# Cached keys of an attention step turned by VectorE in square blocks instead of by TensorE

## The chip, the cores and the metric

The kernel runs on one core of a Trainium2 chip. The metric is the device time of one execution in microseconds (us). The time before is the median of three runs. A profile was recorded by the hardware profiler on one more execution, whose own time is given beside its span. The engines are called PE (TensorE, the matmuls), PEld (its weight loads), DVE (VectorE), ACT (ScalarE), POOL (GpSimd) and SP (the engine that issues most transfers).

## The reference, cut to what matters

One inference step of a hybrid layer: one input projection, whose columns go to eight heads of attention and to a gated short convolution, then an output projection with a residual, then a gated feed-forward part with a residual. 512 new prompt frames and 64 frames of a running stream pass through it. The 64 sample frames also see 512 cached keys and values per head, and only this part of the attention is touched:

```python
# q: (B,Tq,H,Dh), k and v: (B,Tk,H,Dh); 8 heads of 128; 512 cached keys ahead of the 64 new ones
def stick_breaking(q, k, v, q_pos, k_pos):
    z = jnp.einsum('bqhd,bkhd->bhqk', q, k) / math.sqrt(HEAD_DIM)
    mask = (k_pos[None, :] < q_pos[:, None])[None, None]
    log_1mb = jnp.where(mask, jax.nn.log_sigmoid(-z), 0.0)
    after = lax.cumsum(log_1mb, axis=3, reverse=True) - log_1mb
    w = jnp.where(mask, jnp.exp(jax.nn.log_sigmoid(z) + after), 0.0)
    return jnp.einsum('bhqk,bkhd->bqhd', w.astype(v.dtype), v)

k_all = jnp.concatenate([k_past, k], axis=1)     # cache_k: (1, 1, 512 frames, 8 heads, 128)
```

The cached keys lie in memory with the frame as the row. To be multiplied with the queries on TensorE, which contracts over partitions, they must stand with the head's 128 dimensions on the partitions: they have to be turned.

## The kernel before

All matrices are split into a high and a low part (`split`, L228 the cast on ScalarE, L229 the rest on VectorE), and a projection matmul group is three matmuls (`whi` times high, `wlo` times high, `whi` times low).

Attention runs beside the output projection of the convolution's half (`out_proj(mixed_conv, ...)`). Two loops are interleaved. The outer one (`product`, L220) walks over the projection matmuls and calls `pipe.tick()` after every three. The inner one is a Python generator, `attend(h)`, that emits a piece of head h and then yields a number of ticks until its next piece is to be emitted. `heads()` starts a new head every 29 ticks (`PERIOD`), so the end of head h overlaps the start of head h+1.

The order on TensorE is just this order of emission (`manual_schedule` for PE). The order on VectorE, ScalarE, GpSimd and SP is made by the scheduler from dependences and its own cost model, unless `tc.issue_after(x)` holds an instruction behind x.

The pieces of one head, by ticks from its start:

- 0 to 6: the scores `z2`, `z1`, `z0` of the prompt frames against the prompt keys in blocks; on each `softplus` (three ScalarE passes L1131 to L1133 and one VectorE pass L1134 into `pr` or `hbl`), the mask and a running sum on GpSimd (L1189, L1195), and splits into `ph`/`pl`, `s1h`/`s1l`, `s0h`/`s0l`.
- 7: `zs`, the scores of the 64 sample frames (L1204): first one block of new keys from `kf`, then four blocks of cached keys from `kcT`. Behind it `softplus`, and on GpSimd a mask, a copy and three running sums (L1208 to L1212).
- 16: `keys_cached(h + 1)`: TensorE turns the next head's cached keys `cK`, in four 128x128 transposes (matmuls with the identity, L1157) into a PSUM bank `kc`; ScalarE copies the bank to `kcT` (L1158); then the load of the keys after those is issued on SP (`load_cached_keys`, L1042). For head 0 `keys_cached(0)` stands between the scores `z1` and `z0`.
- 18 to 31: the sums over later keys and the weights (`weights`), the split of `sp` into `sph` and `spl` (read by `sample_weights`, L1219, L1220), and the mixed output `po` in PSUM.
- 34, which is tick 5 of the next head: `mixed(po, 0, TP)`. ScalarE makes the high part `hi` of the mixed output and VectorE the low part `lo` (L1274), both parts of the tile `mixa`. ScalarE then squares `po` for the norm.

So TensorE reads `kcT` of head h+1 two ticks behind the last matmul into `po` of head h, and there is one buffer each of `cK` and `kcT`.

## Time and profile before

| | before |
|---|---|
| time, median of 3 runs | 2329.69 us (2328.64 to 2332.22) |
| the profiled execution's own time | 2329.59 us |
| its span in the profile | 2327.9 us |
| PE busy | 2315.9 us (99%) |
| DVE busy | 1956.4 us (84%) |
| ACT busy | 1221.5 us (52%) |
| POOL busy | 298.1 us (13%) |
| granted TensorE clock | 1.00 |
| transfers | 368.57 MB, 158 GB/s in the mean |
| transposes into `kc` on PE | 32, from 584.0 to 716.5 us, 272 ns median |
| copies `kcT` from `kc` on ACT | 8, from 585.6 to 718.1 us, 578 ns median |

The span is the time from the first to the last instruction; the profiled execution's own time has 1.7 us around it. Busy time is the sum over an engine's instructions. Durations of matmuls are modelled and overlap, so what a matmul costs TensorE is read from the distance of the starts. "A <- B" in a row of waits means that A waited for B; "out<-in" in other rows is the tile that an instruction writes and those that it reads.

### The profile page before, as it was taken

Reading aid. Unit: us, or ns where it says so; the run is one execution under the profiler, and the core shown is the slowest. Engines: PE = TensorE matmul, PEld = TensorE weight load, DVE = VectorE, ACT = ScalarE, POOL = GpSimd, SP = SyncE. Lnnn points to the kernel's source line nnn. Section 1 sums busy time; section 2 is a strip of 40 time slices with the busy share of each in tenths; the row PEclk is TensorE's granted clock in tenths of the full one; section 3 lists DMA queues with packets and bytes.
Section 4 is the critical chain, followed back from the end, with each engine's and each line's share of the span. In section 5 each row is a group of like instructions: output and inputs, shape, how many; then the busy total and the mean of one; then the engine's idle time right before and its main releaser. Section 6 shows DMA issues by size and latency. Waiting matters only on the chain.

```text
span 2327.9 us, 43552 instructions
## 1 busy us (share of the span) xinstructions
PE 2315.9 (99%) x17432; PEld 2306.7 (99%) x17432; DVE 1956.4 (84%) x2871; ACT 1221.5 (52%) x2170; POOL 298.1 (13%) x374
## 2 busy tenths in 40 slices
PE   9999999999999999999999999999999999999999
PEld 8999999999999999999999999999999999999999
DVE  8889989897777898888888888888888777887897
ACT  8556656456887564444444444444444444444443
POOL 0211121110332320000000000000000002431222
PEclk9999999999999999999999999999999999999999
DMA  8444343546643454444444444345344936885654
GB/s 272 136 118 130 91 142 109 145 131 209 192 144 108 162 204 127 155 139 140 150 134 150 133 146 155 116 152 158 116 155 136 349 129 211 222 242 186 205 137 100
DMA packets 533770, 368.57 MB, mean 158 GB/s; under 512 B 70278, under 2 KB 518016, under 8 KB 533568
## 3 DMA queue, kind: packets, MB, share of 16 engines
q1 hardware_dynamic: 527072, 356.45, 48.9%
q0 software_dynamic: 6384, 9.21, 2.2%
q8 instruction: 136, 2.23, 0.4%
q14 instruction: 66, 0.54, 0.1%
q10 hardware_dynamic: 112, 0.14, 0.0%
HBM read 285.52 MB, written 80.23 MB: 157 GB/s over the span
## 4 chain that ended last, share of the span: by engine, by line
PE 93%; ACT 3%; DVE 2%; DMA 1%; issue 0%; POOL 0%; SPq 0%; POOLq 0%; ACTq 0%; DVEq 0%
PE psy L405 47%; PE psw L405 23%; PE psx L405 12%; PE pjo L224 6%; PE pj L691 1%; PE pjz L691 1%; PE psv L405 1%; PE pjm L691 1%; DMA raw_a<-in_w_down_dram 0%; ACT ph L228 0%; PE psx L556 0%; ACT whi L176 0%; DVE whl L229 0%; DMA raw_b<-in_w_down_dram 0%; DMA vtok<-v_dram 0%
## 5 line engine op out<-in xcount | busy, mean ns | idle before, releaser
L229 DVE TENSOR_TENSOR whl<-raw_a,whl 128x1024 fp32r<-128x1024 f32 (+4 forms) x384 | 432.8, 1128 | 55.0 <-ACT whl L228 53.4
L405 PE MATMUL psy<-t,whl 128*128 128x288 f32 x3000 | 447.2, 294 | 0.0
L228 ACT CAST whl<-raw_a 128x1024 fp32r<-128x1024 f32 (+4 forms) x384 | 360.0, 939 | 139.9 <-PE psx L405 45.3
L405 PE MATMUL psy<-h_s,whl 128*128 128x288 f32 x2766 | 416.4, 294 | 0.6 <-ACT part L428 0.6
L405 PEld LDWEIGHTS psy<-t,whl 128*128 128x128 f32 x3000 | 414.3, 188 | 0.0
L405 PE MATMUL psw<-t,whl 128*128 128x288 f32 x2688 | 388.9, 294 | 0.0
L405 PEld LDWEIGHTS psy<-h_s,whl 128*128 128x128 f32 x2766 | 383.1, 188 | 0.9 <-ACT part L428 0.8
L405 PEld LDWEIGHTS psw<-t,whl 128*128 128x128 f32 x2688 | 366.7, 188 | 0.0
L228 ACT CAST whl<-raw_b 128x1024 fp32r<-128x1024 f32 (+5 forms) x234 | 211.4, 905 | 209.9 <-issue 71.4
L229 DVE TENSOR_TENSOR whl<-raw_b,whl 128x1024 fp32r<-128x1024 f32 (+5 forms) x234 | 253.2, 1082 | 72.7 <-ACT whl L228 71.6
L428 ACT COPY part<-psy 128x288 f32<-128x288 f32 x309 | 123.2, 399 | 346.6 <-PE psy L405 343.2
L405 PE MATMUL psx<-h_s,whl 128*128 128x288 f32 x1164 | 170.2, 294 | 0.0
L228 ACT CAST whl<-s 128x1024 fp32r<-128x1024 f32 (+5 forms) x103 | 95.3, 925 | 123.5 <-PE psw L405 116.0
L405 PEld LDWEIGHTS psx<-h_s,whl 128*128 128x128 f32 x1164 | 159.6, 188 | 0.0
L405 PE MATMUL psy<-t12a,whl 128*128 128x288 f32 x1056 | 150.5, 295 | 0.0
L405 PE MATMUL psw<-t34a,whl 128*128 128x288 f32 x1056 | 150.4, 295 | 0.0
L405 PEld LDWEIGHTS psy<-t12a,whl 128*128 128x128 f32 x1056 | 143.3, 188 | 0.4 <-ACT part L428 0.2
L405 PEld LDWEIGHTS psw<-t34a,whl 128*128 128x128 f32 x1056 | 143.5, 188 | 0.0
L1454 POOL DMA_DIRECT2D hid_dram<-form x7 | 5.2, 738 | 951.7 <-DVE form L229 944.5
L229 DVE TENSOR_TENSOR whl<-s,whl 128x1024 fp32r<-128x1024 f32 (+5 forms) x103 | 110.4, 1071 | 19.2 <-ACT whl L228 18.2
L224 PE MATMUL pjo<-mixc,whi 128*128 128x288 f32 x512 | 119.0, 300 | 0.0
L224 PE MATMUL pjo<-mixa,whi 128*128 128x288 f32 x512 | 102.8, 296 | 0.0
(565 smaller groups left out, 3920.8 us busy)
## 6 DMA issues: line engine op xcount, KB each, us to landing
hid_dram<-form SPq DMA_DIRECT2D x147, 288.0 KB
raw_a<-in_w_in_dram SPq DMA_DIRECT2D x22, 1024.0 KB
raw_b<-in_w_in_dram SPq DMA_DIRECT2D x22, 1024.0 KB
raw_b<-in_w_gate_dram SPq DMA_DIRECT2D x22, 1024.0 KB
raw_b<-in_w_up_dram SPq DMA_DIRECT2D x22, 1024.0 KB
raw_a<-in_w_gate_dram SPq DMA_DIRECT2D x22, 1024.0 KB
raw_a<-in_w_up_dram SPq DMA_DIRECT2D x22, 1024.0 KB
h_s<-hid_dram SPq DMA_DIRECT2D x10, 2016.0 KB
```

Source lines behind the costliest of these rows:

```text
L224: mm(ps, w_[:, k, csl], x_[:, a:b], start=(k == 0 and n == 0), stop=(k == nk - 1 and n == 2))
L228: cast = nc.scalar.copy(out=hi, in_=src)
L229: (lo_eng or nc.vector).tensor_tensor(out=lo, in0=src, in1=hi.bitcast(F32), op=ALU.subtract)
L405: mm(ps, whl[:, w_, j, :], x_, start=(start and j == 0 and q == 0), stop=(j == len(xs_) - 1 and q == 2), skip_group_check=True)
L428: nc.scalar.copy(out=t, in_=st["y"])
L691: mm(banks_[c][i], w3[:, kt % 8, c * P : (c + 1) * P], t[:, x_, :], start=(kt == 0 and n == 0), stop=(kt == KD - 1 and n == 2))
L1454: q.dma_start(out=hid_dram[fp][2 * n - 2 : 2 * n].rearrange("f p t -> p f t"), in_=t.bitcast(F32))
```

## The change

The keys are loaded in another arrangement. The 512 cached keys of a head are cut into 16 groups of 32 frames and the 128 dimensions into four groups of 32. Row g+j of `cK` holds, for frame j of each of the 16 groups, the 32 dimensions from g on. That takes four transfers per head, each of pieces of 32 numbers (128 bytes), in place of one with pieces of 128 numbers (512 bytes). One VectorE instruction then turns each 32x32 block in itself (`nc.vector.transpose`, a STREAM_TRANSPOSE of 128x512), and what comes out is `kcT` as before. The transposes on TensorE, the bank `kc` and the copy on ScalarE are gone.

The place changes too. For head 0 the keys are turned ahead of the loop over heads. For head h+1 they are turned directly behind VectorE's low part of the mixed output of head h (tick 34 of head h, tick 5 of head h+1), held there by `issue_after`. The load of the next keys stands where `keys_cached` stood.

```diff
-    cK = bpool.tile([P, 4, P], F32, name="cK")
+    cK = bpool.tile([P, TP], F32, name="cK")
...
     def load_cached_keys(h):
-        nc.sync.dma_start(out=cK, in_=ck[:, h, :].rearrange("(i p) d -> p i d", p=P))
+        for g in range(0, P, BK):
+            nc.sync.dma_start(out=cK[g : g + BK].rearrange("j (t d) -> j t d", d=BK),
+                              in_=ck[:, h, g : g + BK].rearrange("(t j) d -> j t d", j=BK))
...
+    nc.vector.transpose(out=kcT, in_=cK)
+
...
-    def keys_cached(h):
-        kc = ps_pj.tile([P, 512], F32, tag="pj", name="kc")
-        for i in range(4):
-            nc.tensor.transpose(kc[:, i * P : (i + 1) * P], cK[:, i, :], ident)
-        nc.scalar.copy(out=kcT, in_=kc)
-        if h + 1 < NH:
-            load_cached_keys(h + 1)
...
             yield 3 if b else 1
-            if h == 0 and b == 1:
-                keys_cached(0)
...
         yield 1
         if h + 1 < NH:
-            keys_cached(h + 1)
+            load_cached_keys(h + 1)
         yield 2
...
         def mixed(ps, a, b):
             nc.scalar.activation(out=hi[:, a:b], in_=ps, func=AF.Copy, scale=ga)
-            nc.vector.scalar_tensor_tensor(out=lo[:, a:b], in0=ps, scalar=ga, in1=hi[:, a:b].bitcast(F32),
-                                           op0=ALU.mult, op1=ALU.subtract)
+            return nc.vector.scalar_tensor_tensor(out=lo[:, a:b], in0=ps, scalar=ga, in1=hi[:, a:b].bitcast(F32),
+                                                  op0=ALU.mult, op1=ALU.subtract).ins
...
-        mixed(po, 0, TP)
+        behind = mixed(po, 0, TP)
+        if h + 1 < NH:
+            with tc.issue_after(behind):
+                nc.vector.transpose(out=kcT, in_=cK)
```

What the change moves on the engines that the scheduler orders is shown at two places. The first is VectorE at the passage from head 1 to head 2. `hbl<-z` is the last pass of a softplus of head 2, `mixa` the low part of head 1's mixed output, `pl` and `s0l` low parts of splits for head 2, `x_2` an output of the projection. Before:

```order
L1134 TENSOR_SCALAR hbl<-z_7309,hbl 128x384
L1274 TENSOR_SCALAR mixa_6730<-po,vec,mixa_6730 128x512
L229 TENSOR_TENSOR pl_6705<-hbl,ph_6704 128x384
L229 TENSOR_TENSOR s0l<-hbl,s0h 128x384
L1104 TENSOR_TENSOR x_2_6737<-pjo,accc 128x288
```

After, at the same place:

```order
L1136 TENSOR_SCALAR hbl<-z_7301,hbl 128x384
L1268 TENSOR_SCALAR mixa_6733<-po,vec,mixa_6733 128x512
L1286 STREAM_TRANSPOSE kcT<-cK 128x512
L229 TENSOR_TENSOR pl_6705<-hbl,ph_6704 128x384
L229 TENSOR_TENSOR s0l<-hbl,s0h 128x384
```

The block transpose has come in between the mixed output and the two splits.

The second place is head 0. On ScalarE, `hbl<-z` and `hbl<-hbl` 128x384 are the softplus passes of key block 1, those on `pr_6700` of key block 0, `hbl<-zs` and `hbl<-hbl` 128x320 those of the sample frames, `whi` weight casts, and `ph_6704`, `ph_6702` and `s0h` the high parts for key block 1, key block 0 and the running sum. Before:

```order
L1131 ACTIVATE hbl<-z_6835 128x384
L1131 ACTIVATE pr_6700<-z_6867 128x512
L1132 ACTIVATE hbl<-hbl 128x384
L1132 ACTIVATE pr_6700<-pr_6700 128x512
L1133 ACTIVATE hbl<-hbl 128x384
L1133 ACTIVATE pr_6700<-pr_6700 128x512
L1131 ACTIVATE hbl<-zs 128x320
L176 COPY whi_6913<-raw_a 128x512
L228 COPY ph_6704<-hbl 128x384
```

After:

```order
L176 COPY whi_6910<-raw_a 128x512 x2
L1133 ACTIVATE hbl<-z_6839 128x384
L228 COPY ph_6702<-pr_6700 128x512
L1134 ACTIVATE hbl<-hbl 128x384
L1133 ACTIVATE hbl<-zs 128x320
L1135 ACTIVATE hbl<-hbl 128x384
L1134 ACTIVATE hbl<-hbl 128x320
L176 COPY whi_6910<-raw_a 128x512
L1135 ACTIVATE hbl<-hbl 128x320
L228 COPY ph_6704<-hbl 128x384
L176 COPY whi_6910<-raw_a 128x512
L228 COPY s0h<-hbl 128x384
```

The softplus of block 1 has moved behind that of block 0 and is interleaved with the sample's, and `ph_6704` and `s0h` stand behind both.

On GpSimd in head 0, L1189 (after: L1185) is the mask, L1195 (L1191) the running sum that `s0h` is cut from, and L1208, L1210 and L1212 (L1202, L1204 and L1206) are the sample's mask, copy and three running sums. Before:

```order
L1189 TENSOR_TENSOR hbl<-hbl,m_6692 128x128
L1189 TENSOR_TENSOR pr_6700<-pr_6700,m_6692 128x128
L1116 DMA x_0_6727<-xt_dram 128x2x576
L1195 TENSOR_TENSOR hbl<-hbl,pr_6701 128x256
L1208 TENSOR_TENSOR hbl<-hbl,s_6694 128x64
L1210 COPY hbl<-hbl 128x64
L1212 TENSOR_TENSOR hbl<-hbl 128x64 x3
```

After:

```order
L1185 TENSOR_TENSOR pr_6700<-pr_6700,m_6692 128x128
L1118 DMA x_0_6730<-xt_dram 128x2x576
L1185 TENSOR_TENSOR hbl<-hbl,m_6692 128x128
L1202 TENSOR_TENSOR hbl<-hbl,s_6694 128x64
L1204 COPY hbl<-hbl 128x64
L1206 TENSOR_TENSOR hbl<-hbl 128x64 x2
L1191 TENSOR_TENSOR hbl<-hbl,pr_6701 128x256
L1206 TENSOR_TENSOR hbl<-hbl 128x64
```

The running sum for `s0h` has moved behind the sample's mask, copy and two of its three sums.

## The prediction

> **What bounds the kernel now.** I read the page first, then the busy time by stage, then TensorE's waits inside the stage that the change touches, then the time line at the places that it moves. The page's head and its chain of waits:

> ```profile
> span 2327.9 us, 43552 instructions
> ...
> PE 2315.9 (99%) x17432; PEld 2306.7 (99%) x17432; DVE 1956.4 (84%) x2871; ACT 1221.5 (52%) x2170; POOL 298.1 (13%) x374
> ...
> PE 93%; ACT 3%; DVE 2%; DMA 1%; issue 0%; POOL 0%; SPq 0%; POOLq 0%; ACTq 0%; DVEq 0%
> ```

> TensorE (PE) is busy for 99% of the span and carries 93% of the chain that ends last. So two things count: matmul time that goes away, and moments in which TensorE has to stand still. Attention runs from about 575 to 750 us. Busy time by stretch (PE, PEld, DVE, ACT, POOL, then clock, DMA share and GB/s); the third row lies in the final stores and is used further down:

> ```profile
> 575.00:605.00 30.00, 29.65 (x219) 29.02 (x218) 20.42 (x41) 22.77 (x50) 7.72 (x14) 1.00 0.95 289
> 605.00:750.00 145.00, 143.22 (x1045) 138.54 (x1044) 109.58 (x232) 116.36 (x264) 50.04 (x92) 1.00 0.42 122
> 2305.00:2310.00 5.00, 5.00 (x40) 5.00 (x39) 5.00 (x8) 2.56 (x5) 1.61 (x2) 1.00 0.20 33
> ```

> Here too TensorE stands still for only 2.1 us of 175, at a granted clock of 1.00, while VectorE (DVE) and ScalarE (ACT) have a quarter of their time free. The waits of TensorE over 575 to 755 us are three rows (total us, times, longest):

> ```profile
> PE zs L1220 <- DVE spl L229: 1.3, 4, 0.4
> PE zs L1204 <- ACT kcT L1158: 0.3, 1, 0.3
> PE zs L1219 <- ACT sph L228: 0.3, 1, 0.3
> ```

> So the cached keys are late once, by 0.3 us, in the first head. In the seven others `kcT` was ready well before its use: no wait for it stands in the view.

> **What it removes.** Eight times four transposes on TensorE and the copy out of PSUM on ScalarE. TensorE's time line around one of the eight (start, duration, operation):

> ```profile
> 590.64 0.30 PE L224 MATMUL pjo<-mixc,whi 128*128 128x288 f32 x1
> 590.78 0.60 PE L1157 MATMUL kc<-ident,cK 128*128 128x128 f32 x4
> 591.13 0.38 PE L224 MATMUL pjo<-mixc,whi 128*128 128x288 f32 x1
> 591.34 0.30 PE L224 MATMUL pjo<-mixc,wlo 128*128 128x288 f32 x1
> ...
> L1158 ACT COPY kcT<-kc x8: 564/578/587, 585.6 to 718.1; 128x512 f32<-128x512 f32 x8
> ```

> A projection matmul takes a slot of 0.14 us (590.64 to 590.78). Without the four transposes the `whi` row would start at 590.78 and the `wlo` row at 590.92; it starts at 591.34. One group costs 0.42 us, eight cost 3.4 us, all on the path: **-3.4 us**. The 0.58 us ScalarE copies (the last row, eight times) are no direct gain, since ScalarE is not what ends last; they loosen the 1.6 us of waits for `sph` and `spl` in the rows above. I take half of that, **-0.8** (bounds 0 and -1.6). In head 0 VectorE turns the keys with no PSUM trip, so the 0.3 us wait goes: **-0.3**.

> **What it adds on VectorE.** Eight block transposes of 128x512. None of that size stands in the trace; the nearest rows are one size below and one above:

> ```profile
> L1607 DVE STREAM_TRANSPOSE acc<-acc x14: 464/469/475, 2272.1 to 2316.8; 128x288 f32<-128x288 f32 x14
> ...
> L807 DVE STREAM_TRANSPOSE tok<-E-18_2212 x1: 769/769/769, 202.6 to 202.6; 128x576 f32<-128x576 f32 x1
> ```

> On the line between 0.469 us at 288 and 0.769 us at 576 columns, 512 columns take 0.70 us (bounds 0.47 and 0.77). Eight are 5.6 us on an engine with room. As busy time they cost nothing. [...]

> **Where the turning now stands.** This is the main term. Before, the keys of head h+1 were turned in the middle of head h. Now VectorE turns them directly behind the mixed output of head h (L1274 in the rows), and TensorE reads `kcT` (L1204) a few slots after the last matmul of that output. Both rows at each of the seven passages from a head to the next:

> ```profile
> 606.63 1.06 PE L1204 MATMUL zs<-qf,kcT 128*128 128x64 f32 x8
> 607.23 0.74 DVE L1274 SCALAR_TENSOR_TENSOR mixa<-po,vec,mixa 128x512 fp32r<-128x512 f32 x1
> 627.00 0.75 DVE L1274 SCALAR_TENSOR_TENSOR mixa<-po,vec,mixa 128x512 fp32r<-128x512 f32 x1
> 627.25 1.06 PE L1204 MATMUL zs<-qf,kcT 128*128 128x64 f32 x8
> 648.66 0.75 DVE L1274 SCALAR_TENSOR_TENSOR mixa<-po,vec,mixa 128x512 fp32r<-128x512 f32 x1
> 648.98 1.06 PE L1204 MATMUL zs<-qf,kcT 128*128 128x64 f32 x8
> 669.38 0.75 DVE L1274 SCALAR_TENSOR_TENSOR mixa<-po,vec,mixa 128x512 fp32r<-128x512 f32 x1
> 669.94 1.06 PE L1204 MATMUL zs<-qf,kcT 128*128 128x64 f32 x8
> 690.79 0.75 DVE L1274 SCALAR_TENSOR_TENSOR mixa<-po,vec,mixa 128x512 fp32r<-128x512 f32 x1
> 691.27 1.06 PE L1204 MATMUL zs<-qf,kcT 128*128 128x64 f32 x8
> 711.64 1.06 PE L1204 MATMUL zs<-qf,kcT 128*128 128x64 f32 x8
> 711.89 0.74 DVE L1274 SCALAR_TENSOR_TENSOR mixa<-po,vec,mixa 128x512 fp32r<-128x512 f32 x1
> 732.17 0.75 DVE L1274 SCALAR_TENSOR_TENSOR mixa<-po,vec,mixa 128x512 fp32r<-128x512 f32 x1
> 732.17 1.06 PE L1204 MATMUL zs<-qf,kcT 128*128 128x64 f32 x8
> ...
> 608.06 0.56 DVE L229 TENSOR_TENSOR pl<-hbl,ph 128x384 fp32r<-128x384 f32 x1
> 732.84 0.42 DVE L229 TENSOR_TENSOR hbl<-pr,hbl 128x256 fp32r<-128x256 f32 x1
> ```

> At every passage the mixed output ends on VectorE after TensorE has begun to read `kcT`. What is queued behind it can only be later. An operation starts 0.08 us before its predecessor's end (732.84 against 732.92), so the keys are turned 0.62 us after the mixed output ends. In the new order that holds for five passages; in the first the `pl` row (ends 608.62) and in the last the `hbl` row (ends 733.26) stand between. TensorE's wait is the turned time less its start above: 609.24-606.63 = 2.61; 628.37-627.25 = 1.12; 650.03-648.98 = 1.05; 670.75-669.94 = 0.81; 692.16-691.27 = 0.89; 713.25-711.64 = 1.61; 733.88-732.17 = 1.71. Together **+9.8 us**. TensorE works in order: behind the waiting matmul are the next head's projection matmuls, and nothing passes it. No group is removed between the `po` matmuls and this read, so TensorE doesn't arrive later by itself. Bounds: 0.23 us less each with the 0.47 us row (8.2), 0.07 us more with the other (10.3); with the mixed output itself earlier by the 0.58 us of the copy that went, 5.7.

> **Head 0 in a new order.** With `kc` gone the planner takes ScalarE's and GpSimd's (POOL's) work of head 0 in another order. Key block 1's softplus and its `ph` cast come behind block 0's, behind two more weight casts, the `zs` pass and the `ph` cast of block 0. The sum that feeds `s0h` comes behind the sample's mask, copy and two running sums. Rows of before:

> ```profile
> 590.36 0.53 ACT L228 CAST ph<-hbl 128x384 fp32r<-128x384 f32 x1
> 591.85 0.60 ACT L176 CAST whi<-raw_a 128x512 fp32r<-128x512 f32 x1
> 593.28 0.51 ACT L228 CAST s0h<-hbl 128x384 fp32r<-128x384 f32 x1
> 594.27 0.34 PE L1247 MATMUL z<-ph,trir 128*128 128x384 f32 x1
> 596.93 0.34 PE L1257 MATMUL z<-s0h,neg1r 128*128 128x384 f32 x1
> ...
> 614.42 0.69 POOL L1208 TENSOR_TENSOR hbl<-hbl,s 128x64 f32<-128x64 f32 x1
> 615.83 1.97 POOL L1212 TENSOR_TENSOR hbl<-hbl 128x64 f32<-128x64 f32 x3
> ```

> `ph` ended at 590.89 and TensorE used it at 594.27: 3.4 us in hand, of which TensorE, earlier by two groups and the first wait, takes 1.2. Five ScalarE instructions of some 0.55 us in front, less the copy of 0.58, take 2.2, all that is left; I book 0.6. `s0h` ended at 593.79 for 596.93, 3.1 us less the same 1.2 = 1.9 in hand; GpSimd's mask, copy and two sums take 2.7 (614.42 to two thirds of the last row, 617.14), and they wait in their turn for the `zs` softplus, so I book 1.4. Together **+2.0** (bounds 0, since ScalarE could run ahead, and 5, if both chains slip by what stands in front in full).

> **The loads.** `cK` now comes in four issues of 128-byte pieces in place of one in 512-byte pieces; qf, kf and vtok stay behind or in front of it on SP. One issue of before:

> ```profile
> 584.62 0.40 SPq L1042 DMA_DIRECT2D cK<-in_cache_k_dram  x1
> ```

> Three more issues hold SP for 1.2 us per head. Small pieces move at 33 GB/s for a share of 0.20, so 165 GB/s (2305 to 2310 us, SP's final stores in 128-byte pieces), the wide traffic of 575 to 605 us at 289/0.95 = 304: 256 KB take 1.6 us in place of 0.9. The next keys are wanted 15 us after their load, at a DMA share of 0.42: nothing.

> **Sum.** -3.4 -0.8 -0.3 +9.8 +2.0 = +7.3 us on the profiled execution's 2329.59 us (span 2327.9 and 1.7 around it), 0.10 below the median of the three runs: **2336.9 us**.

> **The rivals.**
> *Only half the waits.* ScalarE, with one copy fewer, makes each mixed output 0.58 us earlier, and head 0's new order is absorbed: -3.4 -0.8 -0.3 +5.7 = +1.2, 2330.8 us. For it: ScalarE ran into the passages without a pause. Against: the copy stood in the middle of the head, many instructions earlier, with waits for VectorE in between. Chance 0.15.
> *The keys in time (other side).* If VectorE turns them before TensorE arrives, only the removals are left: -3.4 -1.6 -0.3 = -5.3, 2324.3 us. It decides at the passages: the mixed output would have to end 0.8 to 2.6 us earlier than in the rows. A planner that lets ScalarE run ahead could do part of it, the copy's 0.58 us do not reach. Chance 0.07.
> *Keys late from memory.* If the 128-byte pieces take twice my rate or more in head 0, where DMA runs at 0.95, the transpose on VectorE waits for `cK` and holds the softplus of head 0 behind it: 3 to 5 us more, 2340 to 2342 us. Against: `cK` is issued ahead of the scores, and the first read of `kcT` follows them. Chance 0.08. [...]

> **How the numbers follow.** The forecast has 0.70, its own range 2332.5 (waits 8.2, head 0 nothing, relief 1.6: +2.9) to 2341 us (10.3, 5, no relief: +11.6). The first rival's 2330.8 and the third's 2342 are taken in, rounded outwards: 2330.5 to 2343. A difference of 0.2%, 4.7 us, is about what a measurement of this kernel can tell. Slower by more: four fifths of the forecast and all of the third rival, 0.64. Within: the rest of the forecast and the first rival, 0.29. Faster: 0.07.

> **What would show it.** In the changed kernel's profile: no `kc` rows; 128x512 transposes near 0.70 us; TensorE's waits led by `zs` <- VectorE `kcT`, seven times, 0.8 to 2.6 us; in head 0 small waits for `ph` and `s0h`. It is wrong if that wait is missing or under 5 us in all, or if the `kcT` transposes wait for DMA.

## The result, and the profile after

| | before | changed |
|---|---|---|
| median of 7 runs | 2328.94 us (2328.61 to 2332.22) | 2337.68 us (2335.66 to 2337.91) |
| ratio to before, 95% interval | | 1.0033 (1.0024 to 1.0043) |
| profiled execution, own time and span | 2329.59 and 2327.9 us | 2337.91 and 2335.8 us |

The change makes the kernel slower by 8.7 us between the medians and by 7.7 us, 0.33%, between the means. The forecast was 2336.9 us. One execution of a variant below (the reader four ticks later) took 2476.50 us at a granted clock of 0.85, against 2327 to 2329 us of its ten others, and no reading rests on it. The head of the page of the changed kernel and TensorE's waits over 575 to 765 us (total us, times, longest):

```profile
span 2335.8 us, 43521 instructions
PE 2317.6 (99%) x17400; PEld 2307.8 (99%) x17400; DVE 1961.0 (84%) x2879; ACT 1218.0 (52%) x2162; POOL 300.3 (13%) x374
...
PE zs L1198 <- DVE kcT L1286: 6.2, 7, 1.7
PE zs L1198 <- DVE kcT L1152: 0.5, 1, 0.5
PE z L1251 <- ACT s0h L228: 0.4, 1, 0.4
PE zs L1214 <- DVE spl L229: 0.4, 1, 0.4
PE z L1252 <- DVE s0l L229: 0.2, 1, 0.2
```

The wait that was forecast leads the list, seven times, 6.2 us in all. TensorE has 32 instructions fewer and is still busy 1.7 us longer than before, which no wait can explain. The seven waits one by one (start, duration, operation, in brackets the idle time before it), and the turn itself:

```profile
610.00 1.93 PE L1198 MATMUL zs<-qf,kcT 128*128 128x64 f32 x8 [1.69 <-DVE kcT L1286]
633.43 1.10 PE L1198 MATMUL zs<-qf,kcT 128*128 128x64 f32 x8 [0.17 <-DVE kcT L1286]
655.61 1.10 PE L1198 MATMUL zs<-qf,kcT 128*128 128x64 f32 x8 [0.97 <-DVE kcT L1286]
677.17 1.10 PE L1198 MATMUL zs<-qf,kcT 128*128 128x64 f32 x8 [0.98 <-DVE kcT L1286]
699.16 1.10 PE L1198 MATMUL zs<-qf,kcT 128*128 128x64 f32 x8 [0.29 <-DVE kcT L1286]
720.29 1.10 PE L1198 MATMUL zs<-qf,kcT 128*128 128x64 f32 x8 [1.00 <-DVE kcT L1286]
741.61 1.10 PE L1198 MATMUL zs<-qf,kcT 128*128 128x64 f32 x8 [1.12 <-DVE kcT L1286]
...
L1286 DVE STREAM_TRANSPOSE kcT<-cK x7: 700/703/705, 609.2 to 740.8; 128x512 f32<-128x512 f32 x7
```

The turn takes 0.70 us, as read from the two rows beside its size. The first row shows something else: eight matmuls that take 1.06 us at every passage of before and 1.10 us at the six others here take 1.93 us. The next view says why: busy time by stretch behind the first and the fourth passage (us, PE busy, granted clock, DMA share, GB/s).

```profile
608.00:609.00 1.00, 0.32 (x4) 1.00 0.10 29
609.00:610.00 1.00, 0.00 (x0) 1.00 0.71 196
610.00:611.00 1.00, 0.99 (x5) 0.54 1.07 321
611.00:612.00 1.00, 1.00 (x6) 0.50 0.15 45
...
615.00:616.00 1.00, 1.00 (x6) 0.50 1.26 210
616.00:617.00 1.00, 1.00 (x6) 0.55 0.40 56
617.00:618.00 1.00, 1.00 (x10) 1.00 0.05 7
...
678.00:682.00 4.00, 4.00 (x21) 4.00 (x21) 2.53 (x6) 3.13 (x10) 2.16 (x4) 0.57 0.90 238
```

TensorE stands still for 1.69 us, comes back at half clock and stays there from 610.1 to 616.9 us. In those microseconds 5 or 6 matmuls are done in place of 10. Summed as one less the clock, that is 0.46 + 5 x 0.50 + 0.45 = 3.4 us lost. Behind the fourth passage (the last row, a view of all engines, in which the clock is the third number from the end) it is 4 x 0.43 = 1.7 us. So the stand-stills have a second price, **5.1 us at half clock**, nearly as large as the waits themselves. Busy time hides it (1.00 us busy of each 1.00 at a clock of 0.50); the clock column shows it.

### The profile page after: what moved, and what is told of

Same layout as the page of the kernel before. It is cut to its first block, busy times and chain, and to the rows that moved or that the text cites. A ratio compares the mean times of both kernels' runs of the same rounds, so it can differ in the third digit from the quotient of the medians.

```text
span 2335.8 us, 43521 instructions
## 1 busy us (share of the span) xinstructions
PE 2317.6 (99%) x17400; PEld 2307.8 (99%) x17400; DVE 1961.0 (84%) x2879; ACT 1218.0 (52%) x2162; POOL 300.3 (13%) x374
## 4 chain that ended last, share of the span: by engine, by line
PE 92%; ACT 4%; DVE 2%; DMA 1%; POOL 1%; issue 1%; POOLq 0%; DVEq 0%; ACTq 0%; SPq 0%
PE psy L405 47%; PE psw L405 24%; PE psx L405 12%; PE pjo L224 6%; PE psv L405 1%; PE pjz L691 1%; PE pjm L691 1%; ACT ph L228 0%; ACT whi L176 0%; DMA raw_a<-in_w_down_dram 0%; DMA xt_dram<-st 0%; ACT pr L1225 0%; DVE hbe L229 0%; ACT hbe L228 0%; ACT pr L1134 0%
## 5 line engine op out<-in xcount | busy, mean ns | idle before, releaser
L229 DVE TENSOR_TENSOR whl<-raw_a,whl 128x1024 fp32r<-128x1024 f32 (+4 forms) x384 | 433.3, 1129 | 54.5 <-ACT whl L228 52.0
L228 ACT CAST whl<-raw_a 128x1024 fp32r<-128x1024 f32 (+4 forms) x384 | 360.1, 939 | 138.9 <-PE psx L405 44.4
L228 ACT CAST whl<-raw_b 128x1024 fp32r<-128x1024 f32 (+5 forms) x234 | 211.3, 905 | 208.0 <-issue 71.4
L229 DVE TENSOR_TENSOR whl<-raw_b,whl 128x1024 fp32r<-128x1024 f32 (+5 forms) x234 | 253.9, 1085 | 73.4 <-ACT whl L228 71.8
L228 ACT CAST whl<-s 128x1024 fp32r<-128x1024 f32 (+5 forms) x103 | 95.3, 925 | 124.1 <-PE psw L405 116.6
L229 DVE TENSOR_TENSOR whl<-s,whl 128x1024 fp32r<-128x1024 f32 (+5 forms) x103 | 110.4, 1072 | 19.4 <-ACT whl L228 18.4
L224 PE MATMUL pjo<-mixc,whi 128*128 128x288 f32 x512 | 120.7, 306 | 0.0
L224 PE MATMUL pjo<-mixa,whi 128*128 128x288 f32 x512 | 102.8, 295 | 0.0
```

The costliest lines, as they stand in the source:

```text
L224: mm(ps, w_[:, k, csl], x_[:, a:b], start=(k == 0 and n == 0), stop=(k == nk - 1 and n == 2))
L228: cast = nc.scalar.copy(out=hi, in_=src)
L229: (lo_eng or nc.vector).tensor_tensor(out=lo, in0=src, in1=hi.bitcast(F32), op=ALU.subtract)
```

## The experiments

The theory taken to the chip (A): the loss is the seven waits and the half clock that follows some of them. The rivals: (B) the 128-byte pieces of the load cost the time, (C) the scheduler's new order in head 0 does. All ratios are to the kernel before, run on the same chip, whose median there was 2328.9 to 2329.4 us.

**The turn moved earlier.** VectorE's turn behind the masking at tick 18, the load one head ahead:

```diff
+                masked = nc.vector.scalar_tensor_tensor(out=zb[i][:, :P], ..., in1=mneg, ...).ins
+            if b == 2 and h + 1 < NH:
+                with tc.issue_after(masked):
+                    nc.vector.transpose(out=kcT, in_=cK)
+                if h + 2 < NH:
+                    load_cached_keys(h + 2)
...
-            with tc.issue_after(behind):
-                nc.vector.transpose(out=kcT, in_=cK)
```

> The changed kernel with the turn of the next head's keys moved from behind the mixed output (tick 34) to behind the masking in weights(2) (tick 18 of the head before), and the load one head ahead as it was before the change. Theory A (the loss is TensorE's wait for kcT at seven passages, 6.2 us in the trace, and the half clock behind two of them, about 5.0 us): both go, the removed transposes stay removed, 2337.7 - 11.2 = 2326.5 us, so about 2.5 us faster than before. Theory B (the 128-byte pieces cost the time): it stays at 2335 us or more, since the loads are the same. Theory C (the scheduler's new order in head 0 costs most): it stays above 2333 us, since head 0 has no better order here.

Measured: 2330.36 us, ratio 1.0002 (0.9994 to 1.0011). The 8 us are gone with the pieces as small as before, which B does not allow. But 2326.5 was missed. TensorE's waits and one stretch with its clock, of this kernel:

```profile
PE z L1244 <- ACT ph L228: 1.9, 1, 1.9
PE zs L1199 <- DVE kcT L1152: 0.5, 1, 0.5
...
594.00:601.00 7.00, 4.93 (x22) 4.37 (x21) 4.29 (x9) 4.20 (x10) 2.90 (x7) 0.76 1.08 307
```

No wait for a turn of L1228 is left. In head 0 `ph` of key block 1 is later still than in the changed kernel: 1.9 us of waiting, and 7 x 0.24 = 1.7 us at half clock behind it. Put against the kernel before, matmul by matmul (explained under "Why the prediction was right"), head 0 costs TensorE 4.0 us here and 2.1 us in the changed kernel, which is 1.9 of this run's shortfall of 3.9 us. The rest is not assigned; TensorE's waits for `sph` and `spl` are 1.6 us here and 0.4 us in the changed kernel. Here a stand-still for quite another reason, 1.92 us for `ph`, had the same second price, 1.7 us.

**The turn not held.** At the same place in the code, but free for the scheduler:

```diff
-            with tc.issue_after(behind):
-                nc.vector.transpose(out=kcT, in_=cK)
+            nc.vector.transpose(out=kcT, in_=cK)
```

> The changed kernel with the turn emitted at the same place but not held behind the mixed output on VectorE, so that the scheduler may put it earlier (its order puts six of the seven turns ahead of the mixed output, most of them many instructions ahead). Theory A: most of the wait and of the half clock go, 2326.5 to 2330 us. Theories B and C: no change from 2337 us.

Measured: 2329.88 us, ratio 1.0002 (0.9993 to 1.0011). Its trace has no wait for a turn of L1285. The row of TensorE's waits with the largest sum, and the stretch with the seven passages (us, PE, PEld, DVE, ACT, POOL, clock, DMA share, GB/s):

```profile
PE zs L1214 <- DVE spl L229: 1.7, 4, 0.6
...
605.00:750.00 145.00, 142.13 (x1024) 136.69 (x1023) 112.73 (x239) 113.29 (x259) 50.65 (x93) 1.00 0.50 134
```

No half clock is left at the passages. The loads are those of the changed kernel, at the same place, and so is the turn in the code: one `issue_after` decides over the 8 us.

**The reader moved later.** The turn stays behind the mixed output; TensorE's `zs` pass comes two or four ticks later:

```diff
-            yield 3 if b else 1
+            yield 3 if b else 5        # four ticks; 3 for two ticks
...
-        yield 8
+        yield 4                        # 6 for two ticks
```

> The changed kernel with the turn left behind the mixed output, but TensorE's zs pass emitted four ticks (twelve projection matmuls, about 1.6 us) later, at tick 11 instead of 7; the wait after it is four ticks shorter. Theory A: the longest wait was 1.7 us, so nearly all waits and the half clock go: 2326.5 to 2329 us. Theories B and C: 2337 us.

> The changed kernel with TensorE's zs pass two ticks later (six projection matmuls, 0.8 us). Theory A with the clock: some 1.5 us of the 6.2 us of waits are left, and no stand-still is long enough for the half clock: 2337.7 - 4.7 - 5.0 = 2328 us. Theory A without the clock (the half clock is not caused by the waits and stays): 2333 us.

Measured: 2328.14 us with four ticks, ratio 0.9992 (0.9983 to 1.0001); 2329.16 us with two, ratio 1.0000 (0.9991 to 1.0009). A second run with four ticks, for its profile:

> The changed kernel with TensorE's zs pass four ticks later, once more, for the profile: no wait for kcT over 0.3 us, no half clock in the attention stage, head 0's waits for s0h and s0l (0.6 us) still there, span about 2326.5 us.

It took 2329.07 us with a span of 2327.0 us. There was no half clock in the stage, as expected. But TensorE waited for `kcT` up to 0.9 us, 1.4 us in all, where 0.3 at most was expected, and in head 0 it waited 1.1 us for `ph` in place of the waits for `s0h` and `s0l`. Why was not tried. The kernel with two ticks says most about the clock. Its waits and its clock from 605 to 760 us:

```profile
PE zs L1198 <- DVE kcT L1286: 4.2, 6, 1.0
...
605.00:760.00 155.00, 150.55 (x1098) 146.62 (x1097) 119.85 (x256) 120.11 (x276) 49.98 (x92) 1.00 0.53 144
```

It still waits 4.2 us, more than the 1.5 that I expected, but never longer than 1.0 us at once, and the clock stays at 1.00. Against the changed kernel 2.0 us of waits went, and 8.5 us of time. With the 5.1 us of half clock that makes 7.1; the other 1.4 us are not assigned. The clock is the larger part of the difference: had it stayed without the waits, 2333 us were expected.

**The turn made twice.** Another transpose behind the first at each passage:

```diff
                 nc.vector.transpose(out=kcT, in_=cK)
+                nc.vector.transpose(out=kcT, in_=cK)
```

> The changed kernel with each of the seven turns behind the mixed output made twice, so that the keys come 0.62 us later at each passage. If waits alone cost time (theory A without the clock): waits 6.2 + 4.3 = 10.5 us, 2342.0 us. If longer stand-stills of TensorE also halve its clock more often (theory A with the clock): half clock behind more than the two passages it had, 1.7 to 3.4 us each, so 2344 us or more, with a granted clock under 1.00 in four or more stretches. If the waits are incidental: about 2338 us.

Measured: 2345.84 us, ratio 1.0071 (1.0057 to 1.0085). TensorE's waits and its clock behind the passages:

```profile
PE zs L1198 <- DVE kcT L1287: 11.3, 7, 2.5
...
611.00:617.00 6.00, 5.04 (x27) 5.04 (x28) 3.76 (x9) 4.01 (x11) 1.63 (x5) 0.72 0.77 204
636.00:640.00 4.00, 4.00 (x21) 4.00 (x20) 2.91 (x6) 3.53 (x10) 1.42 (x2) 0.57 0.93 238
680.00:684.00 4.00, 3.90 (x19) 3.90 (x20) 2.87 (x8) 3.15 (x10) 2.11 (x4) 0.57 0.70 208
704.00:708.00 4.00, 4.00 (x21) 4.00 (x21) 3.08 (x8) 2.88 (x9) 1.70 (x3) 0.57 0.95 256
728.00:732.00 4.00, 4.00 (x21) 4.00 (x20) 3.37 (x8) 2.21 (x7) 2.04 (x4) 0.57 0.79 181
```

Five stretches at half clock in place of two, each costing 1.7 us: 8.6 us against 5.1 (one of the two was twice as long). With waits longer by 5.1 us that makes +8.6 us over the changed kernel; 8.2 was measured between the medians. Waits alone, longer by these 5.1 us, would have given 2342.8.

**The loads alone.** The kernel before, with only its load in 128-byte pieces (and `cK` as one tile of 128x512, turned in four slices):

```diff
-        nc.sync.dma_start(out=cK, in_=ck[:, h, :].rearrange("(i p) d -> p i d", p=P))
+        for g in range(0, P, BK):
+            nc.sync.dma_start(out=cK[g : g + BK].rearrange("j (t d) -> j t d", d=BK),
+                              in_=ck[:, h, g : g + BK].rearrange("(t j) d -> j t d", j=BK))
```

> The kernel before with only its loads of the cached keys changed to the four transfers of 128-byte pieces; the transposes on TensorE then turn wrongly arranged keys, which leaves the time of every instruction as it was. Theory A: within 1.5 us of before, 2329 to 2330.5 us. Theory B: 2333 us or more, with waits for cK or with a slower neighbouring transfer.

Measured: 2330.24 us, ratio 1.0002 (0.9993 to 1.0011). So the new loads with all that they bring cost at most 0.11%, and TensorE waits for no `cK`: B, small pieces that come late, falls. The 64 matmuls that read the keys so arranged take 275 ns in the median, as in the kernel before. But they do bring something. TensorE's first read of `kcT` in head 0 and its first matmul for the sample's output, and on ScalarE the last softplus pass of block 0 and the first of block 1:

```profile
586.88 1.10 PE L1206 MATMUL zs<-qf,kcT 128*128 128x64 f32 x8 [0.74 <-ACT kcT L1160]
607.32 1.00 PE L1299 MATMUL zs<-ws,cV 128*128 128x64 f32 x8
...
588.23 0.64 ACT L1135 ACTIVATE pr<-pr 128x512 f32<-128x512 f32 x1
588.76 0.49 ACT L1133 ACTIVATE hbl<-z 128x384 f32<-128x384 f32 x1
```

ScalarE's softplus of block 1 stands behind that of block 0 here too, as in the changed kernel, although the transposes and the copy are still there. And head 0 takes 20.44 us between the two rows of TensorE, as in the changed kernel, which saves 0.4 us of transposes in between; in the kernel before it takes 18.75 (rows under the next heading). So the form of the loads alone is enough for a new order on ScalarE and for a loss of 1.7 us in head 0, of which 0.9 us come back in the next two heads, where TensorE waits less. So B and C are not apart: as far as this trace shows, what the loads cost comes with the scheduler's order and not from late keys.

**Head 0 as before.** The other seven heads as changed:

```diff
-    load_cached_keys(0)
+    nc.sync.dma_start(out=cK.rearrange("p (i d) -> p i d", d=P), in_=ck[:, 0, :].rearrange("(i p) d -> p i d", p=P))
...
             yield 3 if b else 1
+            if h == 0 and b == 1:
+                kc = ps_pj.tile([P, 512], F32, tag="pj", name="kc")
+                for i in range(4):
+                    nc.tensor.transpose(kc[:, i * P : (i + 1) * P], cK[:, i * P : (i + 1) * P], ident)
+                nc.scalar.copy(out=kcT, in_=kc)
...
-    nc.vector.transpose(out=kcT, in_=cK)
```

> The changed kernel with head 0 alone as it was before the change (its keys in one load of 512-byte pieces, turned by TensorE, copied by ScalarE), which gives ScalarE and GpSimd back their old order in head 0; the other seven heads are as in the changed kernel. If head 0's new order costs what the trace shows (2.3 us between head 0's scores and its sample output): 2337.7 - 2.3 + 0.4 for the four transposes = 2335.8 us, waits at the passages unchanged. If head 0 costs nothing: 2338.1 us.

Measured: 2333.86 us, ratio 1.0020 (1.0011 to 1.0029), lower than expected. Its waits at the passages are about those of the changed kernel, 6.6 us in all and 1.9 us at the longest. But half clock followed only that longest one and cost 1.7 us (610.0 to 613.5 us), so 3.4 us of it went too, which the expectation did not have. Head 0's own price is read from where TensorE first reads `kcT` and where it begins the sample's output; rows of before, of the changed kernel and of this one:

```profile
586.20 1.10 PE L1204 MATMUL zs<-qf,kcT 128*128 128x64 f32 x8 [0.35 <-ACT kcT L1158]
604.95 1.00 PE L1297 MATMUL zs<-ws,cV 128*128 128x64 f32 x8
```
```profile
586.03 1.10 PE L1198 MATMUL zs<-qf,kcT 128*128 128x64 f32 x8 [0.47 <-DVE kcT L1152]
606.47 1.00 PE L1294 MATMUL zs<-ws,cV 128*128 128x64 f32 x8
```
```profile
586.66 1.10 PE L1201 MATMUL zs<-qf,kcT 128*128 128x64 f32 x8 [0.72 <-ACT kcT L1196]
604.99 1.00 PE L1297 MATMUL zs<-ws,cV 128*128 128x64 f32 x8
```

18.75, 20.44 and 18.33 us. With its old order head 0 loses 2.1 us less. So C is right in kind, but with 2.1 of the 8.7 us it is the smaller part. This run puts back both the load of head 0 and its transposes, so it does not say which of the two makes the order. Where the 2.1 us arise in the changed kernel's head 0:

```profile
593.75 0.44 PE L1241 MATMUL z<-ph,trir 128*128 128x384 f32 x1
594.35 0.44 PE L1242 MATMUL z<-pl,trir 128*128 128x384 f32 x1
...
596.20 0.74 POOL L1191 TENSOR_TENSOR hbl<-hbl,pr 128x256 f32<-128x256 f32 x1
...
597.53 0.44 PE L1251 MATMUL z<-s0h,neg1r 128*128 128x384 f32 x1 [0.44 <-ACT s0h L228]
598.12 0.44 PE L1252 MATMUL z<-s0l,neg1r 128*128 128x384 f32 x1 [0.15 <-DVE s0l L229]
...
603.38 0.34 PE L1172 MATMUL z<-qh,kh 128*128 128x384 f32 x1
603.55 0.34 PE L1172 MATMUL z<-qh,kl 128*128 128x384 f32 x1
```

Two matmuls of this size start 0.17 us apart when nothing is late (the last two rows). By that `pl` is 0.4 us late and `s0l` too, and `s0h` waited 0.4 us by its bracket: the running sum on GpSimd, now behind most of the sample's instructions, ended only at 596.94. These three gaps come to 1.3 us of the 2.1.

**Versions that keep only the gain.** Head 0 as before in each; the turn at tick 18 (best1), or the turn held behind the mixed output and the reader four ticks later (best2), or best1 with `sample_weights` a tick later (best3):

```diff
# best1: the edits of "Head 0 as before" and "The turn moved earlier"
# best2: the edits of "Head 0 as before" and "The reader moved later", four ticks
# best3: best1 and
-                yield 3
+                yield 4
                 sample_weights()
             elif i == 1:
-                yield 3
+                yield 2
```

> Head 0 as before the change and, for the other heads, VectorE's turn at tick 18 of the head before, with the load one head ahead. If the removed matmul time is real time on the path (seven groups of 0.42 us) and the loss was only the passages and head 0: 2329.3 - 2.9 = 2326.4 us. If the gain is used up by longer waits for sph and spl: 2328 to 2329.3 us.

> Head 0 as before the change, the turn behind the mixed output as in the changed kernel, and TensorE's zs pass four ticks later. If head 0's order costs 2.3 us there too: 2328.1 (zs four ticks later alone) - 2.3 + 0.4 = 2326.2 us, no wait for kcT over 0.3 us and no half clock. If the later zs pass moves the waits to sph and spl: 2328 us.

> The best version so far (head 0 as before, turn at tick 18, 2327.6 us) with sample_weights one tick (three projection matmuls, 0.4 us) later, behind which TensorE waited 2.3 us for sph and spl. If those waits are what ate half of the removed 2.9 us: 1.2 to 2 us less, 2325.6 to 2326.4 us. If they only shift to the next reader: 2327.6 us.

Measured: 2327.60 us, ratio 0.9993 (0.9984 to 1.0001); 2327.58 us, ratio 0.9992 (0.9983 to 1.0000); 2328.66 us, ratio 0.9998 (0.9989 to 1.0007). They are 1.3, 1.8 and 0.8 us ahead of the kernel before, and all three intervals reach 1.0000 or beyond: none is shown to be faster. best1 lies between its two forecasts and best3 above both of its own. best2 still waits for `kcT`, 1.8 us in all and 0.8 at the longest, where 0.3 at most was expected. The waits of best1, then of best3:

```profile
PE zs L1218 <- DVE spl L229: 1.4, 3, 0.6
PE zs L1217 <- ACT sph L228: 0.9, 3, 0.3
PE z L1170 <- DVE kl L229: 0.5, 2, 0.3
```
```profile
PE zs L1297 <- ACT ws L1223: 1.3, 2, 1.0
PE zs L1218 <- DVE spl L229: 1.0, 3, 0.4
```

In best1 TensorE waits 2.3 us for `sph` and `spl`, 1.6 us before. Matmul by matmul against the kernel before, the seven groups gave TensorE 3.1 us and the first read of `kcT` 0.5 us, and the other reads, those of `sph`, `spl` and `kl` above all, took 1.4 us back: 2.2 us ahead where attention ends. Moving the reader (best3) made a new wait for `ws`, a step later in the same chain. From 605 to 760 us VectorE is busy 121.5 and ScalarE 119.7 of the 155 us in best1, less than 80%, but their chain is barely ahead of TensorE: with seven groups of transposes fewer, TensorE waits 0.7 us more for it.

## Why the prediction was right, point by point

The time, its direction and its main mechanism, seven waits behind the mixed output, came out as forecast. That the sum came within 0.8 us is luck: the waits at the passages and those for `sph` and `spl` were smaller than forecast, and half clock, which the prediction does not have, filled the gap.

What each place cost can be read from the two traces. Apart from the 32 transposes, both kernels issue the same 17400 matmuls on TensorE in the same order. The start of one of them in the changed kernel's trace, less its start in the trace of before, says how far TensorE is behind by then: 3.37 us at the first passage (610.00 for 606.63), 9.44 us at the last (741.61 for 732.17). Ahead of attention it is 0.1 us, at the last matmuls 7.9 us. It grows and shrinks at these places (us):

| place | forecast | found |
|---|---|---|
| the eight groups of transposes, gone | -3.4 | -3.5 |
| from head 1 on, between the other places: mostly reads of `sph`, `spl` and `ws` | -0.8 | -3.0 |
| the first read of `kcT` in head 0 | -0.3 | +0.1 |
| the seven reads of `kcT` at the passages | +9.8 | +7.4 |
| head 0, from that first read to the sample's output | +2.0 | +2.1 |
| half clock behind the first and the fourth passage | none | +4.7 |
| sum | +7.3 | +7.8 |

The seven waits come to 6.2 us in brackets and to 7.4 us here, because a bracket counts from the modelled end of the matmul before, and the next would have started 0.16 us ahead of that end (0.30 us long in a slot of 0.14). The half clock comes to 5.1 us by the clock and to 4.7 us by the starts.

- **-3.4 (removed matmuls).** Right, 0.44 us for each group. Where nothing holds TensorE up, part of it is lost again to later waits (best1).
- **-0.8 (waits for `sph` and `spl`).** Mis-sized, and not for the reason given. The copies that went were to loosen this chain. In "The turn not held" and in best1, where they went too (in best1 for seven heads) and no passage holds TensorE up, the waits for `sph` and `spl` are 2.6 and 2.3 us, more than the 1.6 of before. They fell in the changed kernel, to 0.4, where TensorE came late to them.
- **-0.3 (first wait for `kcT`).** Wrong: it is 0.47 us, before 0.35. The keys were there 0.17 us sooner (586.03 for 586.20), but TensorE, without the four transposes in front, came 0.29 us sooner.
- **+9.8 (the passages).** Mis-sized: 7.4 us by the same measure. The seven places and the size of the turn were right, and no matmul passed the one that waited (none starts from 609 to 610 us); what the prediction took over from before, how long after the last matmul into `po` the mixed output ends, was not. It ended sooner by 0.8, 0.8, 0.5, 0.5 and 0.5 us at the first, second, fifth, sixth and seventh passage, and 0.0 and 0.3 us later at the third and fourth. At the second and the fifth a half clock stands in front (from 610.1 and from 678.3 us), and my reading is that the other engines catch up in it: the fifth waited 0.29 us, and 0.79 us in "Head 0 as before", where no half clock stands in front of it. Why the other three were sooner stays open. Head 0's delay is little of it: with head 0 as before the first passage still waits 1.89 us, here 1.69.
- **+2.0 (head 0).** 2.1 us; the chains named, `ph`/`pl` and `s0h`, hold most of it. The reason given, `kc` gone, is not needed for it: "The loads alone" keeps `kc`, and has ScalarE's new order and a loss of 1.7 us.
- **Missing: half clock.** I took the clock as 1.00 because the rows of before say so, and they hold no stand-still over 0.4 us in this stage.

The three rivals. "Only half the waits" was half right: the mixed output did end sooner, by 2.8 us over the seven passages. But the copy that went is not shown as the reason: in "The turn not held", which also lacks it, only the first two passages are sooner (0.8 and 0.2 us). And head 0's new order was not absorbed. "The keys in time" did not come about in this kernel. "Keys late from memory" did not either: no turn waits for `cK`, and with all that they bring the small pieces alone cost at most 0.11%.

## What to carry to other kernels

A producer that is off the busiest engine must still be placed by the time at which that engine reads its output: here an instruction of 0.70 us, put behind the last late event ahead of its reader, cost seven waits, and the same instruction half a head earlier cost none. Price a new stand-still of TensorE at its length plus the half clock that may follow (here 1.7 us, once 3.4), and read the clock column by the microsecond, since busy time hides it. When matmuls are taken from a full TensorE, look at how far the chains that feed it are ahead: in best1 1.4 of 3.6 us went back where they became late. And look at the scheduler's order after an edit of a transfer too: here four loads in place of one went with another order on ScalarE and 1.7 us in one head.
